# Branch products amid a chunked scan: an order written out by hand, one bank per chunk, decays from bfloat16 parts

## The chip, the cores and the metric

The kernel runs on one core of a Trainium2 chip. The metric is device time in microseconds for one execution. Before the change three runs took 2236.68, 2237.7 and 2242.37 us; the median is 2237.7. The engines go by their short names: PE is TensorE (PEld its weight loads), DVE VectorE, ACT ScalarE, POOL GpSimd, SP SyncE, whose queue issues the DMAs.

## What is computed

One layer of a hybrid decoder trunk on a sequence of 1024 positions and 1024 channels in float32. Three token mixers read one normalised input; each output goes through its own projection, the three are merged by sigmoid gates, an output projection follows, then a gated MLP.

```python
        y_ssm = ssm_mixer(z, xbc, dt_raw, ...)
        y_sb = stick_breaking_attention(sb_qkv)
        y_nsa = nsa_attention(nsa_q, nsa_kv, nsa_gate, ...)
        gm = jax.nn.sigmoid(merge_gate.astype(jnp.float32)).reshape(bsz, s, 3, D_MODEL)
        mixed = (gm[:, :, 0] * (y_ssm @ w_br_ssm[l]) + gm[:, :, 1] * (y_sb @ w_br_sb[l])
                 + gm[:, :, 2] * (y_nsa @ w_br_nsa[l])).astype(x.dtype)
        x = x + rms_norm(mixed @ w_out[l], post_mix_norm[l])
```

The first mixer's core is a scan over 8 chunks of 128 positions, with 16 heads in 4 groups that share B and C:

```python
    def step(state, inp):
        x_c, dt_c, b_c, c_c = inp
        acum = jnp.cumsum(dt_c * a, axis=1)
        seg = acum[:, :, None] - acum[:, None, :]
        decay = jnp.exp(jnp.where(tri, seg, -jnp.inf))
        cb = jnp.einsum('btgn,bsgn->btsg', c_c, b_c)
        w = cb[..., None] * decay * dt_c[:, None]
        y = jnp.einsum('btsgh,bsghp->btghp', w, x_c)
        y = y + jnp.einsum('btgn,bghpn->btghp', c_c, state) * jnp.exp(acum)[..., None]
        to_end = jnp.exp(acum[:, -1:] - acum) * dt_c
        state = (state * jnp.exp(acum[:, -1])[..., None, None]
                 + jnp.einsum('bsgh,bsghp,bsgn->bghpn', to_end, x_c, b_c))
        return state, y
```

Then a skip term D·x, a gate by silu(z), and a root-mean-square norm over each group's 256 channels.

## The kernel before

Activations lie with channels on the partitions and time on the free axis, in tiles of 128 x 512 or 128 x 1024. A large product of float32 data is made of three: both sides are split into a high part (rounded to fp32r) and the rest, and hi·hi, hi·lo and lo·hi add up in one PSUM bank. For a weight, ACT makes `whi` and POOL `wlo` (L287, L292, columns in pieces of 256). All products pass through two helpers at L219, so in the profile they share a line and are told apart by their tiles.

A scheduler decides the order of instructions on each engine at build time. Where `E.in_order[0]` is set, PE's products keep the order of the program; a `Fill` is a chain of branch or gate products of which `take(n)` writes out n steps at that point.

The stages follow each other: input projections into DRAM rows `s_d`; sparse attention (NSA), at whose end (L1103 to L1121) the scan's decays are made; stick-breaking attention (SB) with the last gate products amid it (`g_d`, written by SP from `gate_e`); `ssd_stage`; `tail_stage` with the branch projections, the output product and the MLP.

`ssd_stage` runs a `scan(q)` for each of the four groups; SSD_AT starts q = 0, 1 at slots 0 and 1, q = 2, 3 at 8 and 9, so that two scans run at a time. In a slot each running scan does `front(c+1)` and `back(c)`:

- `front` (L1294): a decay product `pseg` over 16 rows of fp32r (`half`, two parts of the cumulated decays, by `sel`), a bfloat16 product that adds the mask (`mask_d`), four ACT Exp with a bias (`dec`); transposes of x0, x1 and B, and B·C, into one ps_t bank; DVE `xd`, ACT `Bc`, POOL W = dec * Bc.
- `back` (L1318): C·state over 256 columns, which DVE turns into `yi` (times `eac`); Bc·xd for the new state; POOL and DVE update `state`; four W·xd of 64 x 128 and two ident·yi into the output bank; DVE adds D·x in place. State and output have a bank each (ps_b and ps_o for even q, two of the "dense" tag for odd).
- `norm` (L1346), after chunk 4 and at the end: POOL multiplies by the silu of z, ACT squares, POOL adds the two rows, a product with ones over 512 columns makes the mean square on all partitions, ACT and DVE make the root on 512 columns, and the result goes to `y_d` in DRAM.

No other products are written between these. The three branches come after (L1440). For NSA (rows 12 to 15 of `y_d`), SB (8 to 11) and SSM (0 to 7), each weight block j is loaded once for both halves of the sequence, and `ge`, a block of the gates, is loaded from `g_d`. NSA's result is kept in `lo` tiles, SB's is added by POOL (L1457), and the SSM rows come back from `y_d`.

## Time and profile before

| | us |
|---|---|
| median of 3 runs | 2237.7 |
| lowest, highest | 2236.68, 2242.37 |
| profiled execution, time | 2243.74 |
| profiled execution, span | 2242.0 |
| mean granted TensorE clock | 0.990 of full |
| HBM traffic over the span | 103 GB/s |

Times in the traces are counted from the span's start. In a row of groups stand line, engine, operation, output and inputs by the program's names, shapes, the count, busy time, the mean of one in ns, and the idle time just before them with what ended it. Matmuls overlap in the engine: a row's duration is longer than the distance to the next start. In a timeline row `x8` means eight instructions in a run, and a float32 product outside fp32r takes two instructions.

### The profile page before, as it was taken

How to read it: one execution, taken by the hardware profiler on the slowest of the kernel's cores; microseconds unless marked ns; L12 is line 12 of the kernel's file. 1: busy time of each engine (PE TensorE's matmuls, PEld its weight loads, DVE VectorE, ACT ScalarE, POOL GpSimd, SP SyncE). 2: the span in 40 equal slices, each digit the busy share in tenths (PEclk: the TensorE clock that was granted, in tenths of full speed). 3: DMA queues.
4: the chain of work that ended last, by engine and by line, in shares of the span. 5: the costliest groups of instructions: out<-in, count | busy, mean ns of one | idle time of the engine just before them, and what ended most of it. 6: DMA issues, size and time to landing. Idle time of an engine off the chain costs nothing.

```text
span 2242.0 us, 30070 instructions
## 1 busy us (share of the span) xinstructions
PE 2169.5 (97%) x10589; PEld 1733.7 (77%) x10589; DVE 1309.8 (58%) x2419; ACT 1199.5 (54%) x2236; POOL 1258.4 (56%) x1106
## 2 busy tenths in 40 slices
...
GB/s 174 82 113 108 111 130 61 111 83 36 41 88 36 11 59 38 63 60 65 123 209 69 85 239 145 85 109 176 117 92 80 118 94 109 100 193 171 141 105 117
DMA packets 119527, 232.53 MB, mean 104 GB/s; under 512 B 28752, under 2 KB 43024, under 8 KB 119376
## 3 DMA queue, kind: packets, MB, share of 16 engines
...
HBM read 167.00 MB, written 63.57 MB: 103 GB/s over the span
## 4 chain that ended last, share of the span: by engine, by line
PE 82%; DVE 5%; ACT 4%; POOL 3%; issue 3%; DMA 2%; SPq 0%; DVEq 0%; ACTq 0%; POOLq 0%
PE dense L219 56%; PE ps_s L219 7%; PE ps_o L219 7%; PE ps_t L219 6%; PE ps_b L219 4%; PE psn L219 2%; POOL wlo L538 0%; DMA wraw<-in_wfm 0%; ACT wT L1000 0%; POOL wlo L292 0%; DMA traw<-in_wtm 0%; DMA lo<-m_d 0%; POOL h_lo L472 0%; DVE x L1532 0%; DVE u L329 0%
## 5 line engine op out<-in xcount | busy, mean ns | idle before, releaser
L292 POOL TENSOR_TENSOR wlo<-wraw,whi 128x256 fp32r<-128x256 f32 x328 | 261.3, 827 | 281.5 <-ACT whi L287 270.2
L219 PE MATMUL dense<-h_hi,whi 128*128 128x512 f32 x656 | 262.6, 400 | 0.0
L219 PE MATMUL dense<-h_hi,wlo 128*128 128x512 f32 x656 | 256.8, 392 | 1.1 <-POOL wlo L538 1.1
L219 PE MATMUL dense<-h_lo,whi 128*128 128x512 f32 x656 | 256.7, 391 | 0.0
L1011 POOL TENSOR_TENSOR wT_lo<-wT,wT_hi 128x512 fp32r<-128x512 f32 x132 | 168.6, 1287 | 87.5 <-ACT wT_hi L1010 77.8
L219 PE MATMUL dense<-hi,whi 128*128 128x512 f32 x576 | 214.8, 392 | 0.3 <-ACT whi L287 0.3
L219 PE MATMUL dense<-hi,wlo 128*128 128x512 f32 x512 | 201.8, 396 | 0.4 <-POOL wlo L292 0.4
L219 PE MATMUL dense<-x,uhi 128*128 128x512 f32 x600 | 191.2, 391 | 2.9 <-ACT uhi L546 1.5
L219 PE MATMUL dense<-lo,whi 128*128 128x512 f32 x448 | 175.8, 393 | 0.0
L287 ACT ACTIVATE whi<-wraw 128x1024 fp32r<-128x1024 f32 (+1 forms) x90 | 88.4, 982 | 147.1 <-PE dense L219 117.7
L547 POOL TENSOR_TENSOR ulo<-uf,uhi 128x1024 fp32r<-128x1024 f32 x38 | 92.0, 2421 | 115.3 <-ACT uhi L546 113.4
L219 PEld LDWEIGHTS dense<-h_hi,wlo 128*128 128x128 f32 x656 | 123.2, 188 | 27.9 <-POOL wlo L538 1.5
L219 PEld LDWEIGHTS dense<-h_hi,whi 128*128 128x128 f32 x656 | 123.7, 189 | 23.4
L219 PEld LDWEIGHTS dense<-h_lo,whi 128*128 128x128 f32 x656 | 123.5, 188 | 22.7
L219 PEld LDWEIGHTS dense<-x,uhi 128*128 128x128 f32 x600 | 112.3, 188 | 28.3 <-ACT x L610 2.4
L1215 POOL TENSOR_TENSOR s_lo<-sa,s_hi 128x512 fp32r<-128x512 f32 (+2 forms) x48 | 53.6, 1118 | 139.8 <-ACT s_hi L1214 139.8
L219 PEld LDWEIGHTS dense<-hi,whi 128*128 128x128 f32 x576 | 108.4, 188 | 24.6 <-issue 1.4
L972 DVE TENSOR_REDUCE mx<-ps_t 128x1 f32<-128x384 f32 (+3 forms) x192 | 98.6, 520 | 49.3 <-PE ps_t L219 46.4
L329 DVE SCALAR_TENSOR_TENSOR u<-dense,pv,u 128x511 f32<-128x511 f32 (+1 forms) x140 | 103.4, 741 | 35.2 <-ACT u L325 35.1
L219 PEld LDWEIGHTS dense<-hi,wlo 128*128 128x128 f32 x512 | 96.6, 189 | 23.4 <-issue 1.9
L550 POOL TENSOR_TENSOR ulo<-uf,uhi 128x1024 fp32r<-128x1024 f32 x38 | 91.7, 2414 | 39.6 <-ACT uhi L549 37.8
L1000 ACT ACTIVATE wT<-ps_s 128x512 f32<-128x512 f32 x132 | 78.3, 595 | 60.5 <-PE ps_s L219 56.3
...
## 6 DMA issues: line engine op xcount, KB each, us to landing
wraw<-in_wfm SPq DMA_DIRECT2D x62, 512.0 KB, 3.7
wraw<-in_wup SPq DMA_DIRECT2D x50, 512.0 KB, 3.6
...
ge<-g_d SPq DMA_DIRECT2D x24, 512.0 KB, 3.4
...
row<-s_d SPq DMA_DIRECT2D x16, 512.0 KB, 4.6
```

What stands on the lines that cost most here:

```text
L219: i = f(*a, **k)
L287: act(hi, raw, AF.Copy)
L292: (V if tiles else P).tensor_tensor(lo[:, s], raw[:, s], fl(hi[:, s]), op=OP.subtract)
L329: V.scalar_tensor_tensor(o[:, d:], ps[:, :512 - d], taps[d], o[:, d:], op0=OP.mult, op1=OP.add)
L547: P.tensor_tensor(l24, f24, fl(h24), op=OP.subtract)
L550: P.tensor_tensor(l31, f31, fl(h31), op=OP.subtract)
L972: V.tensor_reduce(mx[:, h, a, n:n + 1], pm[:, :w], axis=AX, op=OP.max)
L1000: act(w.rearrange("p h q -> p (h q)"), pz, AF.Exp)
L1011: P.tensor_tensor(lo, wf, fl(hi), op=OP.subtract)
L1215: (P if SB_SLO else V).tensor_tensor(s_lo[:, c0:], a[:, c0:], fl(s_hi[:, c0:]), op=OP.subtract)
```

## The change

**Branch units inside the scan.** The 32 units of NSA and SB (two branches, two halves, eight blocks j) become a `Fill` of `ssd_stage`; PE keeps the program's order through the whole stage. From slot 1 on, two steps of it (k = two of four, six products) stand behind each front and each back. A weight block is loaded for each half, so 32 times instead of 16. The outputs go to ps_s.

**A chunk's outputs in one bank.** For c > 0 ACT makes exp of the decays over 512 columns, POOL multiplies it by C (`ce`), and four products state·ce of 64 x 128 go straight into the output bank before the four dec·xd; the state update has the bank's other half. `yi`, C·state and ident·yi go.

**Decays in bfloat16.** The cumulated decays are split into three bfloat16 parts (24 rows), so `pseg` is one bfloat16 product; no mask product: a Relu on ACT bounds the exponent, and DVE multiplies B·C by the triangle. DVE, not POOL, makes dec * Bc.

**Norms.** The sums over channels become products with one column of ones, the root is made on 128 x 4, spread by ACT and brought back by four transposes; result and split stay in SBUF (`E.ys`) in row and third tiles. `norm` falls into three pieces, of which the second and third come one and two slots later.

**SSM branch.** It stays behind the scan, by pairs of j and halves. SSD_ROWS sets the slots at which the rows of q = 2, 3 are loaded, in half tiles.

In the diff the removed lines of `ssd_stage` are left out; they stand in the kernel above.

```diff
+SSD_FROM = 1
+SSD_FILL = 2, 2
+SSD_LATE = 1, 0
+SSD_ROWS = {3: [(2, range(4), (0,))], 5: [(3, range(4), (0,))], 7: [(2, range(4), (1,)), (3, range(4), (1,))],
+            11: [(2, (4, 5), (0, 1)), (3, (4, 5), (0, 1))]}
...
-    ac_d = scratch("ac_d", [2, 8, 16, 128])
-    sel = keep.tile([16, 8], R32, name="sel")
-    V.tensor_tensor(sel, ident[0:16, 0:8], ident[0:16, 8:16], op=OP.add)
+    ac_d = dram.tile([3, 8, 16, 128], BF, name="ac_d", tag="ac_d")
+    sel = keep.tile([24, 8], BF, name="sel")
+    V.tensor_tensor(sel, ident[0:24, 0:8], ident[0:24, 8:16], op=OP.add)
+    V.tensor_tensor(sel, sel, ident[0:24, 16:24], op=OP.add)
...
-    act(E.nac.rearrange(fc), ps[:, :128], AF.Copy, scale=-1.0)
+    act(E.acu.rearrange(fc), ps[:, :128], AF.Copy)
...
+    tr(ps[:, 384:512], E.acu.rearrange(fc), ident)
+    ac = wk.tile([128, 128], F32, name="ac", bufs=1)
+    act(ac, ps[:, 384:512], AF.Copy, scale=-1.0)
+    for n in range(3):
+        b = wk.tile([128, 128], BF, name="ab", bufs=3)
+        act(b, ac, AF.Copy)
+        nc.sync.dma_start(E.ac_d[n].rearrange("c h t -> (c h) t"), b)
+        if n < 2:
+            V.tensor_tensor(ac, ac, b, op=OP.subtract)
...
         def front(c):
...
+            h, cs = c // 4, slice(c % 4 * 128, (c % 4 + 1) * 128)
+            pseg = E.ps_d()
+            mm(pseg, E.sel[:, c:c + 1].to_broadcast([24, 128]), ac, start=True, stop=True)
+            dec = wk.tile([128, 4, 128], F32, name="dec", bufs=3)
+            for n in range(4):
+                act(dec[:, n], pseg[:, n * 128:(n + 1) * 128], AF.Relu,
+                    bias=E.acu[:, c, 4 * q + n:4 * q + n + 1])
+            df = dec.rearrange("p h t -> p (h t)")
+            act(df, df, AF.Exp, scale=-1.0)
+            ce = None
+            if c > 0:
+                ce = ce_t()
+                act(ce.rearrange("p h t -> p (h t)"), pseg, AF.Exp, scale=-1.0)
+                P.tensor_tensor(ce, ce, C[h][:, None, cs].to_broadcast([128, 4, 128]), op=OP.mult)
             pt = ps_t()
             for n in range(2):
...
+                tr(pt[:, n * 128:(n + 1) * 128], xs[n][h][:, cs], ident)
+            tr(pt[:, 256:384], B[h][:, cs], ident)
+            mm(pt[:, 384:512], B[h][:, cs], C[h][:, cs], start=True, stop=True)
+            Bc = wk.tile([128, 2, 128], F32, name="Bc", bufs=3)
+            V.tensor_tensor(Bc[:, 1], pt[:, 384:512], E.tri_i, op=OP.mult)
+            act(Bc[:, 0], pt[:, 256:384], AF.Copy)
+            xd = wk.tile([128, 2, 4, 64], F32, name="xd", bufs=3)
             V.tensor_tensor(xd, pt[:, None, :256].rearrange("p a (h d) -> p a h d", h=4).to_broadcast([128, 2, 4, 64]),
                             E.dte[:, :, c, hs, None].to_broadcast([128, 2, 4, 64]), op=OP.mult)
...
+            V.tensor_tensor(dec, dec, Bc[:, 1:2, :].to_broadcast([128, 4, 128]), op=OP.mult)
+            return c, h, cs, xd, dec, ce, Bc
+        def back(c, h, cs, xd, W, ce, Bc):
+            bank = (ps_o if q % 2 else ps_b)()
+            po = [bank[(n % 2) * 64:(n % 2 + 1) * 64, (n // 2) * 128:(n // 2 + 1) * 128] for n in range(4)]
             if c > 0:
...
+                for n in range(4):
+                    mm(po[n], state[:, n, :], ce[:, n, :], start=n < 2, stop=False, skip_group_check=True)
+            for n in range(4):
+                mm(po[n], xd[:, 0, n, :], W[:, n, :], start=c == 0 and n < 2, stop=True, skip_group_check=True)
             if c < 7:
...
+                pst = bank[:, 256:512]
+                mm(pst, Bc[:, 0, :], xd[:, 1].rearrange("p h d -> p (h d)"), start=False, stop=True,
+                   skip_group_check=True)
                 if c == 0:
                     V.tensor_copy(sf, pst)
                 else:
                     P.tensor_tensor(state, state, E.eend[:, c, hs, None].to_broadcast([128, 4, 64]), op=OP.mult)
                     V.tensor_tensor(sf, sf, pst, op=OP.add)
...
             for n in range(2):
...
+                x = xs[n][h][:, cs]
+                V.scalar_tensor_tensor(x, x, pvc(PV_D, 2 * q + n), bank[:, n * 128:(n + 1) * 128],
                                        op0=OP.mult, op1=OP.add)
         def norm(h):
...
+            zs = [held[q][n][h] for n in (4, 5)]
             for n, z in enumerate(zs):
...
+                P.tensor_tensor(xs[n][h], xs[n][h], z, op=OP.mult)
+                act(z, xs[n][h], AF.Square)
+            later.append([SSD_LATE[0], sums, h, zs])
+        def sums(h, zs):
+            ps = ps_t()
+            for m, n in itertools.product(range(4), range(2)):
+                mm(ps[:, m:m + 1], zs[n][:, m * 128:(m + 1) * 128], E.ones[:, 0:1], start=n == 0, stop=n == 1)
+            r = wk.tile([128, 4], F32, name="r")
+            E.rsqrt_mean(r, ps[:, 4:8], ps[:, 0:4], 256)
+            rb = zs[0]
+            act(rb.rearrange("p (n t) -> p n t", t=128), r[:, :, None].to_broadcast([128, 4, 128]), AF.Copy)
+            later.append([SSD_LATE[1], out, h, zs, ps])
+        def out(h, zs, ps):
+            for m in range(4):
+                ms = slice(m * 128, (m + 1) * 128)
+                tr(ps[:, ms], zs[0][:, ms], ident)
+            for n, z in enumerate(zs):
+                V.scalar_tensor_tensor(z, xs[n][h], pvc(PV_SSM, 2 * q + n), ps, op0=OP.mult, op1=OP.mult)
+                hi, lo = [(E.third_t if q % 2 else E.row_t)(R32) for _ in range(2)]
+                act(hi, z, AF.Copy)
+                V.tensor_tensor(lo, z, fl(hi), op=OP.subtract)
+                E.ys[2 * q + n, h] = hi, lo
...
         for c in range(8):
             new = front(c + 1) if c < 7 else None
+            yield
             back(*st)
-            if c == 4:
-                norm(0)
+            if c % 4 == 3:
+                norm(c // 4)
             yield
             st = new
-        norm(1)
+            for x in list(later):
+                x[0] -= 1
+                if x[0] < 0:
+                    later.remove(x)
+                    x[1](*x[2:])
...
+    def rows(k0, h):
+        out = []
+        for k in range(4):
+            hi, lo = [yb.tile([128, 512], R32, name="y", bufs=16) for n in range(2)]
+            nc.sync.dma_start(fl(lo), E.y_d[(k0 + k) * 128:(k0 + k + 1) * 128, E.hs(h)])
+            act(hi, fl(lo), AF.Copy)
+            V.tensor_tensor(lo, fl(lo), fl(hi), op=OP.subtract)
+            out.append((hi, lo))
+        return out
...
+    def branches(ys):
+        units = [(br, h, j) for br in (2, 1) for h in range(2) for j in range(8)]
+        def load(br, h, j):
+            return E.load_w(A["wb_nsa" if br == 2 else "wb_sb"][j], 512)
+        ahead = [load(*units[0])]
+        ys = [ys]
+        for n, (br, h, j) in enumerate(units):
+            w = ahead.pop()
+            if n + 1 < len(units):
+                ahead.append(load(*units[n + 1]))
+            if j == 0:
+                y = ys.pop()
+            if j == 3:
+                nxt = {(2, 0): (12, 1), (2, 1): (8, 0), (1, 0): (8, 1)}.get((br, h))
+                ys = [rows(*nxt)] if nxt else []
+            e = E.row_t()
+            nc.sync.dma_start(e, E.g_d[(br * 8 + j) * 128:(br * 8 + j + 1) * 128, E.hs(h)])
+            out = []
+            yield from E.half_unit(Bank(), w, lambda k, _: y[k], 4, h, out)
+            if br == 2:
+                d = E.part[h, j] = E.lo_t(F32)
+                V.tensor_tensor(d, out[0], e, op=OP.mult)
+            else:
+                V.tensor_tensor(e, out[0], e, op=OP.mult)
+                P.tensor_tensor(E.part[h, j], E.part[h, j], e, op=OP.add)
     held = E.ssm
     gens = [None] * 4
...
+    acs = {q: ac_t(q) for q in range(2)}
+    E.ssm_rows(1, range(4), E.third_t, (0,))
+    fill = E.Fill(branches(rows(12, 0)))
+    E.ssm_rows(1, range(4), E.third_t, (1,))
+    E.ssm_rows(1, (4, 5))
+    E.in_order[0] = True
+    n = 0
+    while n == 0 or any(gens):
+        if n in SSD_ROWS:
+            for q, ns, h in SSD_ROWS[n]:
+                E.ssm_rows(q, ns, E.third_t if q % 2 and ns[0] < 4 else E.row_t, h)
         for q, at in enumerate(SSD_AT):
...
+            if n == at:
+                if q > 1:
+                    acs[q] = ac_t(q)
+                gens[q] = scan(q, *[held[q][m] for m in range(4)])
+            if gens[q]:
+                for m in range(2 if n > at else 1):
+                    if next(gens[q], 0) == 0:
+                        gens[q] = None
+                        break
+                    if n >= SSD_FROM:
+                        fill.take(SSD_FILL[m])
+        n += 1
+    E.in_order[0] = False
+    fill.rest()
...
+    for j0 in range(0, 8, 2):
...
+        for h in range(2):
+            for j, w, e in two:
+                ps, = fm_unit(psd, w, lambda k, h: E.ys[k, h], 8, halves=(h,))
...
```

How this moves instructions shows in three places. First PE in the steady scan. A slot of before, where `half,sel` and `ident_b,mask_d` are the decay product and its mask, `W,xd` a head's product, and `row_10833` and `third_11620` the C of the two scans:

```order
L219 MATMUL dense<-xd,Bc 128x256
L219 MATMUL ps_t<-ident,row_10827 128x128
L219 MATMUL ps_t<-ident,row_10829 128x128
L219 MATMUL ps_t<-ident,row_10831 128x128
L219 MATMUL ps_t<-row_10833,row_10831 128x128
L219 MATMUL ps_b<-state,row_10833 128x256
L219 MATMUL dense<-W,xd 64x128 x4
L219 MATMUL dense<-state,third_11620 128x256
L219 MATMUL ps_s<-half,sel 128x512
L219 LDWEIGHTS mask_d
L219 MATMUL ps_s<-ident_b,mask_d 128x512
L219 MATMUL ps_o<-W,xd 64x128 x4
```

The same part now, where `y` are the rows of a branch (whi and wlo its weights) and `ac` the three bfloat16 parts:

```order
L224 LDWEIGHTS sel
L224 MATMUL dense<-ac,sel 128x512
L224 MATMUL ps_t<-ident,row 128x128 x3
L224 MATMUL ps_t<-row 128x128
L224 MATMUL ps_s<-y,whi 128x512 x2
L224 MATMUL ps_s<-y,wlo 128x512
L224 MATMUL ps_s<-y,whi 128x512 x2
L224 MATMUL ps_s<-y,wlo 128x512
L224 MATMUL ps_b<-ce,state 64x128 x4
L224 MATMUL ps_b<-dec,xd 64x128 x4
L224 MATMUL ps_b<-xd,Bc 128x256
L224 MATMUL ps_s<-y,whi 128x512 x2
```

The mix of two scans that the scheduler had made has become one scan's front, six branch products, its back, and six more. The second place is the start of the stage. PE of before, at the last gate products (`h_hi`, `h_lo` with whi, wlo):

```order
L219 MATMUL dense<-h_hi,whi 128x512
L219 MATMUL dense<-h_lo,whi 128x512
L219 MATMUL dense<-h_hi,wlo 128x512
L219 MATMUL ps_s<-half,sel 128x512
L219 LDWEIGHTS mask_d
L219 MATMUL ps_s<-ident_b,mask_d 128x512
L219 MATMUL ps_o<-w_hi,row_10139 128x512
L219 MATMUL ps_o<-w_hi,row_10140 128x512
L219 MATMUL ps_o<-w_lo,row_10139 128x512
L219 MATMUL dense<-h_hi,whi 128x512
L219 MATMUL dense<-h_lo,whi 128x512
L219 MATMUL dense<-h_hi,wlo 128x512
```

And now, at the very last of them:

```order
L224 MATMUL dense<-h_hi,whi 128x512
L224 MATMUL dense<-h_lo,whi 128x512
L224 MATMUL dense<-h_hi,wlo 128x512
L224 LDWEIGHTS sel
L224 MATMUL dense<-ac,sel 128x512
L224 MATMUL ps_t<-ident,row 128x128 x3
L224 MATMUL ps_t<-row 128x128
```

A decay product that stood amid gates and the last SB product (`w_hi`, `w_lo`) now stands behind all gates. SP's queue around the same place, where `third` are rows of the second pair of scans' tiles, `y` the NSA rows and `gate_e` the last gates:

```order
L1250 DMA y_d<-ysb 128x512 x2
L585 DMA g_d<-gate_e 128x512
L687 DMA third<-s_d 128x512 x6
L1421 DMA y<-y_d 128x512
L687 DMA third<-s_d 128x512 x3
L290 DMA wraw<-in_wb_nsa 128x512
L585 DMA g_d<-gate_e 128x512
L687 DMA third<-s_d 128x512 x2
L1421 DMA y<-y_d 128x512
L687 DMA third<-s_d 128x512 x5
L1299 DMA ac<-ac_d 24x512 x2
L1421 DMA y<-y_d 128x512 x6
```

The loads of `ac` for q = 0 and 1 stand behind all sixteen half tiles `third` (the rows of q = 1 and q = 3) and behind the store of the last gates. The third place is the end of the scan on PE, now:

```order
L224 MATMUL ps_o<-ce,state 64x128 x4
L224 MATMUL ps_o<-dec,xd 64x128 x4
L224 MATMUL ps_o<-xd,Bc 128x256
L224 MATMUL ps_t<-ones,row 128x1 x8
L224 MATMUL ps_o<-ce,state 64x128 x4
L224 MATMUL ps_o<-dec,xd 64x128 x4
L224 MATMUL ps_t<-ident,row 128x128 x4
L224 MATMUL ps_t<-ones,row 128x1 x8
L224 MATMUL ps_t<-ident,row 128x128 x4
L224 MATMUL dense<-row,whi 128x512 x2
```

Where NSA's products stood behind the last chunks before, these last chunks and norms now run without branch products between them, and the first SSM product (`dense<-row,whi`) follows the last transposes. Outside the stretch from the end of the SB stage to the SSM branch, the order on every engine is unchanged.

229 lines of the change are left out of this document (72 added, 157 removed).

## The prediction

> **What bounds the kernel now.** I read the page's busy times first, then its chain of work, then windows over the stages that the change touches.
>
> ```profile
> PE 2169.5 (97%) x10589; PEld 1733.7 (77%) x10589; DVE 1309.8 (58%) x2419; ACT 1199.5 (54%) x2236; POOL 1258.4 (56%) x1106
> PE 82%; DVE 5%; ACT 4%; POOL 3%; issue 3%; DMA 2%; SPq 0%; DVEq 0%; ACTq 0%; POOLq 0%
> ```
>
> TensorE is busy for 97% of the span and carries 82% of the chain that ended last; nothing else has more than 5%. So a change pays where it takes products away or closes gaps between them. A busy figure alone can't tell a full engine, since the records of matmuls overlap. The windows (PE, weight loads, DVE, ACT, POOL, each with its count) say more:
>
> ```profile
> core 0: us, PE busy (x) PEld busy (x) DVE busy (x) ACT busy (x) POOL busy (x), PEclk, DMA share, GB/s
> 1158.00:1171.00 13.00, 10.73 (x56) 6.95 (x55) 5.04 (x12) 8.35 (x27) 6.36 (x7) 0.87 1.03 395
> 1171.00:1185.00 14.00, 14.00 (x97) 9.49 (x95) 7.79 (x19) 7.99 (x28) 9.28 (x10) 1.00 0.39 145
> 1185.00:1215.00 30.00, 29.13 (x193) 20.45 (x193) 23.39 (x55) 15.93 (x43) 21.26 (x21) 1.00 0.11 38
> 1215.00:1235.00 20.00, 17.95 (x85) 9.90 (x83) 12.22 (x25) 12.97 (x34) 13.32 (x11) 0.83 0.41 137
> 1235.00:1285.00 50.00, 48.47 (x308) 34.18 (x306) 34.92 (x76) 25.36 (x72) 34.42 (x32) 1.00 0.21 73
> 1285.00:1325.00 40.00, 39.72 (x176) 31.53 (x176) 23.59 (x36) 13.98 (x24) 13.95 (x17) 1.00 0.66 221
> 1325.00:1368.00 43.00, 42.64 (x188) 34.81 (x187) 23.50 (x24) 12.95 (x16) 37.53 (x32) 1.00 0.65 221
> 1368.00:1458.00 90.00, 90.00 (x387) 72.41 (x386) 25.32 (x31) 18.01 (x23) 47.69 (x50) 1.00 0.29 95
> ```
>
> The last row is dense TensorE: 387 products in 90 us, 0.233 us each. The NSA and SB products (1285 to 1368) run almost as densely. The scan's rows do not: the weight loads fall from 80% of the time to 50-70%, and the granted clock to 0.87 and 0.83. The stage to be judged has these ends:
>
> ```profile
> 1144.66 0.49 PE L219 MATMUL ps_s<-half,sel 16*128 16x512 f32 x1
> 1150.65 0.49 PE L219 MATMUL ps_s<-half,sel 16*128 16x512 f32 x1
> ...
> 1158.60 0.39 PE L219 MATMUL dense<-h_hi,wlo 128*128 128x512 f32 x1
> 1161.04 0.50 PE L219 MATMUL ps_s<-half,sel 16*128 16x512 f32 x1 [2.06 <-ACT dec L1302]
> ...
> 1368.62 0.40 PE L219 MATMUL dense<-yhi,whi 128*128 128x512 f32 x1
> ```
>
> The last gate product starts at 1158.60 and ends its turn at 1158.8; the first SSM-branch product starts at 1368.6. Scan plus two branches take **209.8 us**. All that comes earlier, and the SSM branch, the output product and the FFN behind it, keep their work, so the forecast is about these 209.8 us.
>
> **The change, part by part: TensorE's content.** What a product costs is the distance to the next start, not the printed duration:
>
> ```profile
> 1176.36 0.50 PE L219 MATMUL ps_s<-half,sel 16*128 16x512 f32 x1
> 1176.79 0.39 PE L219 MATMUL ps_s<-ident_b,mask_d 128*128 128x512 bf16 x1
> 1177.02 0.38 PE L219 MATMUL ps_t<-ident,row 128*128 128x128 f32 x2
> 1177.23 0.60 PE L219 MATMUL dense<-xd,Bc 128*128 128x256 f32 x2
> 1177.67 0.27 PE L219 MATMUL ps_t<-ident,row 128*128 128x128 f32 x1
> 1177.78 0.39 PE L219 MATMUL ps_t<-row,row 128*128 128x128 f32 x2
> 1178.09 0.66 PE L219 MATMUL dense<-W,xd 128*64 128x128 f32 x8
> 1178.68 0.71 PE L219 MATMUL dense<-ident,yi 128*128 128x128 f32 x4
> ```
>
> From start to start: the decay product over 16 rows 0.43; the bfloat16 mask of the same 512 columns 0.23; a float32 product of 256 columns (two passes) 0.44; a transpose, like any float32 pass of 128 columns, 0.11; four head products W·xd 0.59.
>
> There are 32 chunks (4 groups of 8), of which 28 have a state. Removed: 32 masks (7.4 us); on 32 decay products the step from 0.43 to the mask row's 0.23, since the new one is one bfloat16 pass over 512 columns (6.4); 28 C·state products (28 x 0.44 = 12.3); 28 pairs of ident·yi (four passes, 28 x 0.44 = 12.3); 8 norm sums over 512 columns, by twice the 256-column price 0.88 each (7.0). **45.4 us go.** Added: 28 sets of four ce·state with the shape of W·xd (28 x 0.59 = 16.5); 32 transposes in the norms (3.5); 64 column sums of one column, 128 passes. No row shows these. The lower bound is nothing; the upper is a whole 128-column pass, 0.11 each, 14 us, as weights are loaded for each. I take the middle, 7, because the nearest row loads the same weights but streams 128 columns more. **27 us come; net -18.4** (-25 to -11).
>
> What stays, besides: 384 branch products x 0.233 = 89.5, transposes 96 x 0.11 = 10.6, B·C 32 x 0.22 = 7.0, W·xd 32 x 0.59 = 18.9, state updates 28 x 0.44 = 12.3, and before the change 32 decay products at 0.43, 13.8. With the removed 39.0 (45.4 less the 6.4 already in those 13.8) that is 191; two decay products with their masks lie ahead of the stage (1144.66, 1150.65), so 190. **The stage now loses 209.8 - 190 = 20 us; after it has 171.5 of content and breaks even if it loses 38.**
>
> **The start, about 11.5 us.** The decay products that now hide among the gate products (1144.66, 1150.65) come behind the last of them, and TensorE's order is fixed there, so transposes and fill wait behind them. They need `ac`. In before's timeline SP issues the scan's rows from 1155.91 on; the list of transfers gives KB each and the median us to landing:
>
> ```profile
> 1155.91 5.07 SPq L679 DMA_DIRECT2D third<-s_d  x8
> ...
> third<-s_d SPq DMA_DIRECT2D x8, 512.0 KB, 7.5
> ```
>
> These 4 MB took the queue 7.5 us each to land. SP's new order puts `ac` behind the last gate's store and all 16 half tiles `third`, two `y` and one weight load, 19 transfers of 0.26 MB: 5.0 MB at 0.395 MB/us (first window) are 12.6 us after 1155.9. So `ac` lands near 1168.5, and TensorE, out of gates at 1158.8, stands for 9 to 10. Two more go to the first chunk's chain and a lowered clock (0.87 in this stretch already). Were the queue emptier, the wait would still hold until the last gate's sigmoid, three ACT passes of about 0.65 (L1352 below has their shape) after 1159, so 4 is the lower end; 16 the upper, if `y` lags too.
>
> **The middle, about 8 us.** Fill stands between every front and back, six products or 1.4 us; a chunk's back comes a whole slot after its front, nearly 11 us with two scans. What other engines do per chunk:
>
> ```profile
> L1302 ACT ACTIVATE dec<-ps_s,nac 128x128 f32<-128x128 f32 x128 | 36.4, 373 | 18.3 <-PE ps_s L219 11.4 <-POOL W L1315 6.5
> L1352 ACT ACTIVATE row<-row 128x512 f32<-128x512 f32 x8 | 5.2, 648 | 3.8 <-POOL row L1351 3.8
> L1310 DVE TENSOR_TENSOR xd<-ps_t,dte 128x512 f32<-128x512 f32 x32 | 21.8, 687 | 18.0 <-PE dense L219 10.7 <-PE ps_t L219 5.8 <-PE ps_b L219 1.3
> L1343 DVE SCALAR_TENSOR_TENSOR row<-row,pv,ps_o 128x128 f32<-128x128 f32 x32 | 9.6, 342 | 2.8 <-PE ps_o L219 2.6
> L1315 POOL TENSOR_TENSOR W<-dec,Bc 128x512 f32<-128x512 f32 x32 | 41.5, 1303 | 23.0 <-ACT Bc L1313 13.4 <-ACT dec L1302 9.5
> L292 POOL TENSOR_TENSOR wlo<-wraw,whi 128x256 fp32r<-128x256 f32 x34 | 27.9, 844 | 38.1 <-ACT whi L287 27.1 <-DMA g_d<-gate_e 11.0
> L1457 POOL TENSOR_TENSOR lo<-lo,ge 128x512 f32<-128x512 f32 x16 | 24.4, 1533 | 3.9 <-DVE ge L1455 3.1 <-PE dense L219 0.6
> L1331 POOL TENSOR_TENSOR state<-state,eend 128x256 f32<-128x256 f32 x24 | 14.7, 614 | 15.7 <-PE dense L219 9.9 <-PE ps_b L219 5.8
> L1351 POOL TENSOR_TENSOR row<-row,row 128x512 f32<-128x512 f32 x8 | 11.1, 1404 | 1.1 <-DVE row L1343 1.1
> L1354 POOL TENSOR_TENSOR row<-row,row 128x512 f32<-128x512 f32 x8 | 10.2, 1278 | 0.0
> ```
>
> ACT: four Relu 1.5, two Exp of 512 columns 1.3, a copy about 0.3: 3.1 per chunk. DVE: xd and the decay product 0.69 each, mask and two D terms 0.34 each, state 0.42: 2.8. Two chunks leave both some 5 of 11 us for units and norms, so the front's chain (1.5 + 0.65 + 1.3 for ce) is hidden by its slot; without that cover 3.5 us per chunk would show. A chunk's one bank is free again after two D terms and the state add, 1.1 us, and wanted a slot later. POOL is tighter, as the weights now come once per half: 32 loads in place of 16, their transfers hidden, their splitting doubled. In the scan's first half its ce (in W's place) and states leave time. In the second half, where the SB units run, its order holds 40 wlo, 16 adds, 15 ce, 13 states and 12 norm products: 40 x 0.844 + 16 x 1.533 + 15 x 1.303 + 13 x 0.614 + 12 x 1.404 = 102.7 us, against some 90 of TensorE. Weights are split one unit ahead and stand behind the adds in POOL's queue; TensorE's fixed order waits for them. About six of the twelve us should show, since the norms' POOL work reaches past the last unit; two more I allow the first half. Bounds 2 and 16.
>
> **The end, about 9.5 us.** The fill runs out two backs early, so q3's last chunk and norm have nothing between them: D terms 0.7, two POOL products 2.8, a Square 0.65, the column sums 0.8 (an eighth of the 7 above), two ACT and four DVE operations on four columns (no row shows one so small; at the 0.34 of a 128-column D term 2.0), a spread copy 0.65, transposes 0.45. That is 8 us, and 1.5 for the bare decay chain of the last chunk. The SSM products, fixed behind these transposes, start late. The norms' result stays on chip; the round trip that goes lay beside other work and gains nothing.
>
> **Sum:** 171.5 + 11.5 + 8 + 9.5 = 200.5, against 209.8: **-9.3 us**, the stage ending near 1359. The profiled execution took 2243.7 us (span 2242.0), 6 above the median of 2237.7; on the median's scale that gives 2228.4.
>
> The Trainium skill, "SBUF — State Buffer", section "SBUF: two separate sides", says that a DVE instruction with two SBUF inputs and a GpSimd one exclude each other for a whole instruction. That speaks against moving dec·Bc to DVE. The same 128x512 add on POOL takes 1278 (L1354) and 1533 ns (L1457), which would suit such a rule, though nothing in those rows names the other party. By it, an estimate, 32 new DVE products of 0.69 us would each hold POOL up, 11 us in the second half; the sum would then be about 2238, near POOL's rival below, which stands without it.
>
> **The rivals.**
> *POOL sets the pace of the second half.* If its operations stretch as the adds do (1533 against 1278, a fifth), ce and the norm products add 7 us to 102.7, 20 beyond TensorE's 90; less some 4 that the last norms' work may reach past the units, the middle costs 16, the total is 2236.4. For it: POOL is busy 37.5 of 43 us beside SB units already. Against: TensorE is busy 42.6 of those 43.
>
> *Slower: fixed order turns each late release into a stand.* Before, a late W let other ready products go first; now all, fill included, stand behind it. It decides from a mean of 0.3 us at each of the 64 places where a front or back begins: 64 x 0.3 = 19 in the middle, with start and end 40 in all, over the 38. At 0.4 the time is 2237.7 + (26 + 21 - 38) = 2246. For: scan rows of before lose 20 us even with free choice. Against: 1.4 us of fill per place, a slot of distance.
>
> *All latencies are covered but start and end.* Middle 0, end 8: 2219. For: the branches of before keep TensorE at 99% with POOL at 87%. Against: POOL's 102.7 above.
>
> *The narrow product is no cheaper.* A bfloat16 product over 24 rows keeps the 0.43 of the 16-row one: 6.4 us less gain, 2235. The mask row (0.23, same columns, bfloat16) speaks against.
>
> **How the numbers follow.** Forecast 0.45, POOL 0.2, fixed order 0.2, all covered 0.12, no cheaper 0.03. The range runs from 2212 (all covered, cheap column sums) to 2248 (fixed order at 0.4, a little over). A difference of 0.3%, 6.7 us, is about what a measurement of this kernel tells from none. Faster: 0.4 of the forecast's 0.45 and the covered case, 0.52; same: POOL's, the narrow product's and the forecast's short end, 0.28; slower: fixed order, 0.2.
>
> **What would show it.** Right: the new decay product 0.23 before the next start; first decay product near 1168, standing on a DMA; weight loads around 75% of the time between; SSM products starting near 1359 behind a gap of some 9 us that ends on ACT or POOL. Wrong: a start beyond 1172, waits on POOL wlo all through the SB units, or TensorE idle at every back. Anything that moves after the SSM branch would also make the sum wrong.

## The result, and the profile after

| | before | after |
|---|---|---|
| median, us | 2239.05 (2236.68 to 2242.37, 4 runs) | 2257.89 (2252.55 to 2260.36, 4 runs) |
| ratio, 95% interval | 1 | 1.0080 (1.0055 to 1.0105) |
| profiled execution, us | 2243.74 | 2255.84 |
| last gate product starts | 1158.60 | 1155.71 |
| first SSM product starts | 1368.62 | 1378.40 |
| stage between the two | 210.0 | 222.7 |

The kernel became slower by some 19 us, 0.8%. The forecast of 2228.4 has the wrong sign, and the range up to 2248 misses the time. The profiled execution of before was 4.7 us above its median, so the two profiles differ by 12.1 us only; the stage accounts for all of that (12.7). Gates end 2.9 us earlier, but in kernels with the same code up to there the last gate product starts anywhere from 1155 to 1159. Some 2 us are lost behind the stage: from the first SSM product to the end of the execution before takes 875.1 us and after 877.4 (875.8 to 879.0 in the kernels below that have the same code there). The other 6.7 us of the medians' difference are in no trace; the profiled execution of after lay 2.1 us below its median.

First the busy times from the page of after.

```profile
PE 2162.1 (96%) x10757; PEld 1735.9 (77%) x10757; DVE 1332.0 (59%) x2477; ACT 1228.7 (55%) x2327; POOL 1272.9 (56%) x1126
```

The page says almost nothing: TensorE's busy time fell by 7 us and the span grew by 12. The windows over the stage say where (PE, weight loads, DVE, ACT, POOL, clock, DMA share, GB/s):

```profile
1156.00:1173.00 17.00, 0.36 (x2) 0.10 (x1) 1.39 (x2) 3.60 (x6) 1.40 (x2) 0.58 0.95 331
1173.00:1180.00 7.00, 7.00 (x29) 4.83 (x28) 4.58 (x8) 6.11 (x17) 1.28 (x1) 0.56 0.41 150
1180.00:1350.00 170.00, 170.00 (x1109) 127.25 (x1107) 123.09 (x249) 102.26 (x271) 136.66 (x135) 0.99 0.39 122
1350.00:1378.00 28.00, 19.96 (x137) 16.37 (x138) 16.82 (x39) 13.13 (x32) 17.56 (x17) 0.74 0.21 75
```

Three things are to be seen. TensorE stands for nearly 17 us at the start, and the 7 us behind that run at a clock of 0.56. The 170 us in the middle are full: 170.00 busy, clock 0.99, no stand, POOL busy for 80%. And 8 of the last 28 us are empty, at a clock of 0.74. So the middle waits for nobody, and yet the stage is long.

The start, from the timeline, first PE's rows and then SP's:

```profile
1155.71 0.39 PE L224 MATMUL dense<-h_hi,wlo 128*128 128x512 f32 x1
1172.74 0.60 PE L224 MATMUL dense<-ac,sel 24*128 24x512 bf16 x1 [16.64 <-DMA ac<-ac_d]
1173.28 0.90 PE L224 MATMUL ps_t<-ident,row 128*128 128x128 f32 x3
...
```

```profile
1153.06 5.03 SPq L687 DMA_DIRECT2D third<-s_d  x6
...
1164.51 2.98 SPq L687 DMA_DIRECT2D third<-s_d  x5
1167.82 0.94 SPq L1299 DMA_DIRECT2D ac<-ac_d  x2
1169.13 3.83 SPq L1421 DMA_DIRECT2D y<-y_d  x6
```

Two loads of 24 KB, issued at 1167.82, are what TensorE waits for; they stand behind 16 tiles `third`, and the queue moved 331 GB/s where the forecast had 395 (225 up to 1162, 392 from there to 1172). Six of the `y` rows follow them.

The full middle, from the timeline: a slot of one scan, and behind the "..." of 1267 a norm's column sums.

```profile
1260.68 0.39 PE L224 MATMUL ps_s<-y,wlo 128*128 128x512 f32 x1
1261.00 0.66 PE L224 MATMUL ps_o<-ce,state 128*64 128x128 f32 x8
1261.49 0.61 PE L224 MATMUL ps_o<-dec,xd 128*64 128x128 f32 x8
1262.02 0.70 PE L224 MATMUL ps_o<-xd,Bc 128*128 128x256 f32 x2
1262.37 0.81 PE L224 MATMUL ps_s<-y,whi 128*128 128x512 f32 x2
1263.02 0.39 PE L224 MATMUL ps_s<-y,wlo 128*128 128x512 f32 x1
...
1263.72 0.40 PE L224 MATMUL ps_s<-y,wlo 128*128 128x512 f32 x1
1264.05 0.39 PE L224 MATMUL dense<-ac,sel 24*128 24x512 bf16 x1
1264.36 0.55 PE L224 MATMUL ps_t<-ident,row 128*128 128x128 f32 x3
...
1267.48 0.39 PE L224 MATMUL ps_s<-y,wlo 128*128 128x512 f32 x1
1267.71 1.84 PE L224 MATMUL ps_t<-ones,row 128*128 128x1 f32 x16
1269.41 0.71 PE L224 MATMUL ps_s<-y,whi 128*128 128x512 f32 x2
```

Read the distances between starts, and the array that each product uses (the pair with *). A branch product (`y,wlo`, 128\*128) ahead of the column sums, also 128\*128, takes its 0.23; ahead of `ce,state` (128\*64) it takes 0.32, ahead of the decay product (24\*128) 0.33. The decay product takes 0.31 before the transposes, where the forecast had the mask's 0.23. By these distances a change of the array's shape costs about 0.09; the experiments test that for the decay product. The two passes behind the back's last product take 0.65 (1262.37 to 1263.02) in place of 0.46. And the 16 passes of the column sums take 1.70 us, 0.106 each: as much as a pass with 128 columns.

The end, from the timeline:

```profile
1356.68 2.79 POOL L297 TENSOR_TENSOR wlo<-wraw,whi 128x256 fp32r<-128x256 f32 x4
...
1359.43 3.38 POOL L1367 TENSOR_TENSOR row<-row 128x512 f32<-128x512 f32 x2
...
1363.53 3.14 PE L224 MATMUL ps_t<-ones,row 128*128 128x1 f32 x14 [1.29 <-ACT row L1368]
...
1369.05 2.49 POOL L1367 TENSOR_TENSOR third<-third,row 128x512 f32<-128x512 f32 x2 [3.99 <-DVE third L1360]
...
1372.59 3.15 PE L224 MATMUL ps_t<-ones,row 128*128 128x1 f32 x14 [0.97 <-ACT row L1368]
...
1377.63 1.11 PE L224 MATMUL ps_t<-ident,row 128*128 128x128 f32 x4 [1.90 <-ACT row L1378]
1378.40 1.20 PE L224 MATMUL dense<-row,whi 128*128 128x512 f32 x2
```

Two norms stand bare here, where the forecast had one; the first one's products wait on POOL behind four pieces of a weight's splitting, and at the lowered clock 14 of a norm's 16 passes take 3.1 us.

### The profile page after: what moved, and what is told of

Read it like the earlier page. It is cut to its first block, busy times and chain, and to the rows that moved or that the text cites. A ratio compares the mean times of both kernels' runs of the same rounds, so it can differ in the third digit from the quotient of the medians.

```text
span 2254.1 us, 30683 instructions
## 1 busy us (share of the span) xinstructions
PE 2162.1 (96%) x10757; PEld 1735.9 (77%) x10757; DVE 1332.0 (59%) x2477; ACT 1228.7 (55%) x2327; POOL 1272.9 (56%) x1126
## 4 chain that ended last, share of the span: by engine, by line
PE 84%; DVE 4%; ACT 4%; issue 3%; DMA 3%; POOL 3%; SPq 0%; DVEq 0%; ACTq 0%; POOLq 0%
PE dense L224 54%; PE ps_s L224 10%; PE ps_t L224 7%; PE ps_o L224 6%; PE ps_b L224 4%; PE psn L224 2%; DMA third<-s_d 0%; POOL wlo L543 0%; ACT wT L1010 0%; DMA wraw<-in_wfm 0%; DMA lo<-m_d 0%; POOL h_lo L477 0%; DVE u L334 0%; POOL wlo L297 0%; ACT wT_hi L1020 0%
## 5 line engine op out<-in xcount | busy, mean ns | idle before, releaser
L297 POOL TENSOR_TENSOR wlo<-wraw,whi 128x256 fp32r<-128x256 f32 x360 | 288.5, 830 | 266.7 <-ACT whi L292 266.4
L224 PE MATMUL dense<-hi,wlo 128*128 128x512 f32 x448 | 176.8, 396 | 0.7 <-POOL wlo L297 0.7
L224 PE MATMUL dense<-hi,whi 128*128 128x512 f32 x448 | 175.3, 391 | 0.0
L292 ACT ACTIVATE whi<-wraw 128x1024 fp32r<-128x1024 f32 (+1 forms) x106 | 99.1, 935 | 106.7 <-PE dense L224 85.7
L543 POOL TENSOR_TENSOR wlo<-wraw,whi 128x1024 fp32r<-128x1024 f32 x38 | 92.9, 2444 | 29.7 <-ACT whi L542 29.5
L224 PE MATMUL dense<-hi,uhi 128*128 128x512 f32 x248 | 98.0, 395 | 6.8 <-ACT snap L1625 5.6
```

The costliest lines, as they stand in the source:

```text
L224: i = f(*a, **k)
L292: act(hi, raw, AF.Copy)
L297: (V if tiles else P).tensor_tensor(lo[:, s], raw[:, s], fl(hi[:, s]), op=OP.subtract)
L543: P.tensor_tensor(wlo, raws[0], fl(whi), op=OP.subtract)
```

## The experiments

Every kernel ran in turn with the one before on the same chip; ratios are to that one, with 95% intervals. The first eight ask which part of the stage is long and what it is worth.

**The decay parts loaded early** (`ac` of two scans into lasting memory at the end of the NSA stage):

```diff
-    acs = {q: ac_t(q) for q in range(2)}
+    # at the end of the NSA stage
+    for q in range(2):
+        E.acs[q] = E.ac_t(q)
```

> The two loads of `ac` for the first pair of scans are issued at the end of the NSA stage instead of behind the sixteen loads of `third`; the dead `eac` goes. In the changed kernel's trace TensorE stands 16.8 us (1155.9 to 1172.7) until `ac` lands, and 3 more are lost to a lowered clock. Theory A (the wait is for `ac` alone): the first decay product comes within 1 us of the last gate product and nearly all of it goes, total 15 us or more below the changed kernel (2243 or less). Theory B (the wait is for the whole burst of loads, and `ac` is only the last of it that TensorE meets): after one or two decay products and their transposes TensorE stops again, for `y`, whose first two rows were used by ACT at 1163.9 and 1169.1; the first branch products come near 1170 instead of 1176, and the total falls by 3 to 6 us (about 2253).

Measured: 2256.05, ratio 1.0074 (1.0056 to 1.0092). The first decay product follows the gates at once, at 1155.47, and then TensorE stands for `y`, as PE's timeline of this kernel shows:

```profile
1156.56 0.37 PE L224 MATMUL dense<-ac,sel 24*128 24x512 bf16 x1
...
1164.99 1.52 PE L224 MATMUL ps_s<-y,whi 128*128 128x512 f32 x2 [7.36 <-ACT y L1424]
...
1171.80 0.79 PE L224 MATMUL ps_s<-y,whi 128*128 128x512 f32 x1 [4.86 <-ACT y L1424]
```

The start still loses 18 us: theory B. The small load was only the first thing to come late; the whole burst is too late. The middle has the same products as after. From the 5th to the 29th decay product it takes 147.0 us here and 148.5 in after, where the clock falls to half for 3.4 us near 1232. The 147.0 is what the next kernels without such a dip are to be compared with.

**One row of squares in the norms** (POOL adds two squared rows; 8 column passes in place of 16 per norm):

```diff
+            P.tensor_tensor(zs[0], zs[0], zs[1], op=OP.add)
-            for m, n in itertools.product(range(4), range(2)):
-                mm(ps[:, m:m + 1], zs[n][:, ...], E.ones[:, 0:1], start=n == 0, stop=n == 1)
+            for m in range(4):
+                mm(ps[:, m:m + 1], zs[0][:, ...], E.ones[:, 0:1], start=True, stop=True)
```

> POOL adds the two squared rows first, so a norm takes 8 column-sum passes instead of 16. Theory A (each pass of one column costs as much as a whole 128-column pass, 0.112 us in the trace, bound by its weights): a norm's sums take 0.92 us instead of 1.84, 8 norms give 7.4 us back, 2 more at the end where the clock is low, against about 3 at the end for two more POOL adds of 1.3 us in the bare tail; total 5 to 8 us below the changed kernel (about 2251). Theory B (the sums were cheap and their 21.8 us are waiting): no change in the middle, and the tail longer by the adds, total 0 to 3 us above.

Measured: 2257.80, 1.0074 (1.0059 to 1.0089). From the 5th to the 29th decay product it takes 142.9 us in place of 148.5, or of 147.0 without the dip of the clock. The groups of after and of this kernel between 1180 and 1345 us, after first:

```profile
L224 PE MATMUL ps_t<-ones,row 128*128 128x1 f32 x80 | 9.2, 245 | 0.0
```

```profile
L224 PE MATMUL ps_t<-ones,row 128*128 128x1 f32 x40 | 4.8, 242 | 0.2 <-POOL row L1369 0.2
```

Forty passes less save 4.1 us, 0.10 each, about the 4.4 that their own rows show. So the sums' price is that of full passes, as theory A had it. The gain is lost in the bare end, where POOL has one more operation per norm: from the last `y` product to the first SSM product it takes 30.7 us instead of 25.4.

**Longer fill blocks, half as many:**

```diff
-SSD_FILL = 2, 2
+SSD_FILL = 4, 0
```

> Fill of four steps (12 products) behind each front and none behind each back: the same products, half as many changes between branch products and scan products. Theory A (a change of kind costs TensorE time by itself, about 0.2 us for going in and out, since the first weights of the next kind load only when the product before is done: the last product before a scan product keeps its place 0.32 instead of 0.23 us and the first behind it is longer too): 30 changes fewer, 5 to 6 us less between 1180 and 1350, total about 2252. Theory B (the branch products' 103 instead of 89.5 us are small waits for operands): nothing gained, or a loss, since a back now follows straight on the other scan's work without fill and its waits are no longer covered; total 2257 or more.

Measured: 2255.62, 1.0063 (1.0048 to 1.0078). The stretch of decay products takes 148.7 us, without a dip of the clock and with 12 more branch products in it, 2.8 us of work: some 1 us is gained on the 147.0, where theory A had 5 to 6. So the number of blocks is not what costs: from the last pass of the chunk product `xd,Bc` straight to the decay product the distance is 0.31 too, against 0.22 for such a pass among like ones, and fewer blocks leave the number of shape changes as it was.

**SSM products as fill in the tail:**

```diff
+        for j in range(2):
+            w = E.load_w(A["wb_ssm"][j], 1024)
...
+            yield from E.half_unit(Bank(), w, lambda k, _: E.ys[k, 0], 8, 0, out)
```

> Two SSM units of the first half (48 products, 11 us) are written as further fill behind the NSA and SB units, so the last chunks have products between them; the same products are left out of the SSM branch, their weights are loaded once more. In the changed kernel the stretch from 1350 to 1380 loses 14 us. Theory A (the end is bare latency: POOL products, squares, sums, root, transposes in a row, with the clock falling): the fill covers the wait before the last backs and half of the norms, 6 to 9 us gained, total about 2250; the last norm of q = 3 stays bare, some 7 us. Theory B (POOL, still busy with weights and adds until 1360, is late, and sets the end whatever TensorE does): the last transposes come no earlier than 1376, the 48 products only move in front, and the gain is their 11 us all the same unless POOL's additional splitting (8 pieces, 6 us) delays the norms by as much; then 5 us or less is gained.

Measured: 2264.05, 1.0100 (1.0085 to 1.0115), worse than after. SSM products need the thirds that the last norms make, and the last norm of all still stands bare (PE's timeline of this kernel):

```profile
1391.46 0.59 PE L224 MATMUL ps_t<-ones,row 128*128 128x1 f32 x2 [6.04 <-ACT row L1368]
```

**All loads of the start in a written order** (the first experiment's early `ac`, and the first `y` rows pinned ahead of `third`):

```diff
+            if (k0, h) == (12, 0):
+                tc.keep_in_program_order(i)
...
+    E.load_order[0] = True
+    first = rows(12, 0)
```

> As the run with the early `ac` (it stopped again behind 3 us of work, at `y`: 14.0 us lost up to 1170 and 17.9 to 1190, against 16.8 and 19.8), but the four `y` rows of the first half are issued ahead of all `third`, and the rows of q = 3 keep their place in the program. Theory A (the burst behind which the loads queue is the cause, whichever load is met first): four `y` and eight `third`, 3.1 MB at 0.36 to 0.4 MB/us from 1153, are there by 1161; TensorE loses 3 to 6 us at the start instead of 18 to 20, and the total falls by 12 to 15 us, to about 2243. Theory B (the memory that the SB stage gives back, not the queue, decides when loads begin, or the scans' other rows are late by as much): the loss stays over 12 us and moves to the third or fourth decay product.

Measured: 2254.73, 1.0059 (1.0040 to 1.0078). The start's loss falls from 18 to 12.6, and neither theory fits whole: pinned, the `y` loads stand behind the last gates' store (SP's timeline, then PE's).

```profile
1162.18 0.42 SPq L585 DMA_DIRECT2D g_d<-gate_e  x1
1162.70 1.89 SPq L1425 DMA_DIRECT2D y<-y_d  x4
```

```profile
1169.61 0.80 PE L224 MATMUL ps_s<-y,whi 128*128 128x512 f32 x1 [7.72 <-ACT y L1428]
```

**The norms' gating products on DVE:**

```diff
-                P.tensor_tensor(xs[n][h], xs[n][h], z, op=OP.mult)
+                V.tensor_tensor(xs[n][h], xs[n][h], z, op=OP.mult)
```

> The two products of a norm (y times the silu of z, 128x512) go from POOL to DVE; nothing else differs from the changed kernel. There, the last ce of q = 3 was ready at 1358.6 and POOL began it at 1363.8, behind four pieces of an SSM weight (2.8 us), two norm products (3.4) and the state (1.1). Theory A (POOL's queue sets the end): the last back comes 3 us earlier and the last norm's products, 2 x 0.7 instead of 2 x 1.25, save one more; the first SSM product comes 3 to 5 us earlier counted from the last gate product, total about 2253. Theory B (TensorE's fixed order and the chain of the norm set it, POOL only fills the time): no change of the end, and 11 us more DVE in a middle where DVE is 75% busy cost up to 2 us.

Measured: 2255.37, 1.0070 (1.0055 to 1.0085); the stage 219.8, 2.9 less: 3.7 at the end, less a little at the start. The middle is 148.5 us as in after, each with one dip of the clock, so POOL did not pace it.

**Part of the fill kept back for the end** (one step in place of two behind the backs of eight slots):

```diff
-                        fill.take(SSD_FILL[m])
+                        fill.take(1 if m and 4 <= n < 12 else SSD_FILL[m])
```

> The same products, but behind the backs of slots 4 to 11 one step of fill instead of two, so that 16 steps (48 products, 11 us) are left for the last slots. Theory A (the end is a chain of waits during which TensorE has nothing written): the middle shortens by 11 us, the end grows by less, since its gaps (14 us from 1350 to 1380) take 48 products in; 5 to 9 us earlier, total about 2250. Theory B (POOL is the bound of the end, as in the run with SSM units there, which lost 18 us in spite of its fill): the SB adds and weights now fall into the end as well and push the norms' POOL products back, gain 3 us or less.

Measured: 2258.78, 1.0088 (1.0072 to 1.0105): no gain. The last `y` product starts at 1370.8 instead of 1353.0, and from there to the first SSM product it takes 10.3 us instead of 25.4; the last norm stays bare. But the middle gives up what the end gains. Between 1190 and 1340 us the granted clock is 0.95, against 0.99 in after: it falls to half three times, which costs 7 us instead of 2, and 1.3 us are a wait. Why the clock falls there is not shown.

**The last three together:**

> The three together: loads in order, norm products on DVE, fill kept for the end. If the start, POOL's queue and the bare end are separate causes, the gains add: 13 + 4 + 6 = 23 us less than the changed kernel, about 2234, below the kernel before (2241.7). If the end is one chain that only moves, the sum falls short by the smaller parts: 2240 to 2244.

Measured: 2245.14, 1.0026 (1.0016 to 1.0036, 9 runs). The start now loses 12.7 us and the end, 8.2 us long, some 5; some 5 more are lost in between, 2.2 of them in waits for `xd` and 1.7 at half clock. That is 23 in all, where the forecast allowed 29. Still the stage is 209.6 us long, against 210.0 of before, whose trace lay above its median: by the medians this kernel is 5.4 slower. **A stage that loses less than the forecast allowed is no shorter than the old one: TensorE's content did not fall by 18.4.** The next four ask why.

**The decay product over all 128 rows**, 104 of them zero, else after:

```diff
-    sel = keep.tile([24, 8], BF, name="sel")
+    sel = keep.tile([128, 8], BF, name="sel")
...
-        ac = wk.tile([24, 512], BF, name="ac")
-        nc.sync.dma_start(ac, E.ac_d[...])
+        ac = wk.tile([128, 512], BF, name="ac")
+        V.memset(ac, 0.0)
+        nc.sync.dma_start(ac[:24], E.ac_d[...])
...
-            mm(pseg, E.sel[:, c:c + 1].to_broadcast([24, 128]), ac, start=True, stop=True)
+            mm(pseg, E.sel[:, c:c + 1].to_broadcast([128, 128]), ac, start=True, stop=True)
```

> The decay product takes 128 rows, of which 104 are zeros, instead of 24; nothing else differs from the changed kernel. There the product behind it starts 0.316 us later and it starts 0.329 us after a branch product, where a bfloat16 product of as many columns and the branch products among themselves take 0.23; the long-fill run has shown that the number of fill blocks is not the cause. Theory A (every change of the shape that the array is used in, 128*128 to 24*128 and back, costs 0.09 us, since the weights of the new shape are not loaded behind the running product): both numbers become 0.23, 0.18 us per chunk, 4 to 4.5 us less from the fifth to the twenty-ninth decay product (148.5 us), total 5 to 6 below the changed kernel (about 2252). Theory B (the change between bfloat16 and float32 products costs it): both stay over 0.31, no gain.

Measured: 2250.31, 1.0053 (1.0037 to 1.0068), 7.6 us below after (by the two ratios, 6.0). PE's timeline of this kernel, to be laid beside 1263.72 to 1264.36 of after:

```profile
1259.32 0.40 PE L224 MATMUL ps_s<-y,wlo 128*128 128x512 f32 x1
1259.56 0.39 PE L224 MATMUL dense<-ac,sel 128*128 128x512 bf16 x1
1259.79 0.49 PE L224 MATMUL ps_t<-ident,row 128*128 128x128 f32 x3
```

The product with five times the rows is cheaper: 0.23 instead of 0.31 to the next start, and 0.24 instead of 0.33 ahead of it. The first transpose behind it takes 0.11 instead of 0.17. From the 5th to the 29th decay product it takes 141.4 us instead of the 147.0 of this code without a dip of the clock. The 5.6 are 0.23 for each of 24 chunks, about what the three distances add up to (0.09, 0.09 and 0.06). That is the shape's price by itself.

**All together** (the three, 128 rows, `y` unpinned, and the squares and ones of the norms in bfloat16):

```diff
-                act(z, xs[n][h], AF.Square)
+                act(z.bitcast(BF)[:, :512], xs[n][h], AF.Square)
```

> As the run of three together (2245.1), with decay products over 128 rows, squares and the column of ones in bfloat16 (the squares lose precision, the sums are one pass of bfloat16 each instead of two of float32), and the first `y` loads no longer pinned behind the last gate's store. Expected from the parts: 5.5 for the shape, 64 fewer passes of 0.115 plus whatever a bfloat16 weight load is shorter, 7 to 10, and 3 to 5 at the start (first branch product near 1162 instead of 1166.6, counted from gates that end at 1156.5): 15 to 20 us below it, 2226 to 2230, that is 10 to 14 below the kernel before. If the content is not what the change lost (a rival: the time is lost in waits of other engines that merely move when TensorE gets shorter, POOL's first), it gains 8 or less: 2237 or more.

Measured: 2239.82, 1.0000 (0.9991 to 1.0009, 11 runs); level with before, where 2226 to 2230 had been worked out. In the profiled execution, 3.2 us below the median, the stage is 200.0 us; the part from the first SSM product on takes 878.4, 3 more than before's 875.1. So of the 10 us by which the two traces' stages differ, 3 are lost behind the stage, and the rest is that before's trace lay above its median and this one below. PE's timeline and the waits between 1158 and 1358 us (engine, tile, what it waited for: us, times, longest):

```profile
1253.24 0.35 PE L224 MATMUL ps_t<-ones_b,row 128*128 128x1 bf16 x8
1253.46 0.71 PE L224 MATMUL ps_s<-y,whi 128*128 128x512 f32 x2
```

```profile
PE ps_t L224 <- DVE xd L1342: 9.8, 7, 3.4
PE ps_b L224 <- DVE dec L1344: 5.7, 1, 5.7
PE ps_t L224 <- ACT row L1385: 4.0, 1, 4.0
```

Eight bfloat16 passes take 0.22 us, 0.028 each, against 0.106 for a float32 one. But with TensorE shorter, DVE is late: it now holds the norms' products as well, and TensorE stands for its `xd` seven times.

**The norms' products on POOL again for the first two groups, else the same:**

```diff
-                V.tensor_tensor(xs[n][h], xs[n][h], z, op=OP.mult)
+                (P if q < 2 else V).tensor_tensor(xs[n][h], xs[n][h], z, op=OP.mult)
```

> As the run of all parts together (2239.8), but the norm products of the first pair of scans (q = 0, 1) go back to POOL; those of q = 2, 3 stay on DVE. In that run TensorE waited 9.8 us in seven places for DVE's xd, DVE being 83% busy over the sampled windows, while POOL was 50 to 60% busy between 1230 and 1260. Theory A (DVE had become the bound in places): four of the seven waits, 8.5 us of the losses between 1210 and 1280, go; total 2232 to 2235, below the kernel before by 0.2 to 0.3%. Theory B (the waits come from rows that land late, since the loads are pinned, and DVE only shows the transposes' bank): no gain, 2238 or more.

Measured: 2238.78, 0.9996 (0.9987 to 1.0005, 11 runs). The windows and the waits:

```profile
1200.00:1350.00 150.00, 138.61 (x985) 104.39 (x989) 124.48 (x247) 95.71 (x249) 121.34 (x119) 0.99 0.39 125
```

```profile
PE ps_t L224 <- DVE xd L1342: 9.2, 6, 2.3
```

The wait stayed, so the products of those two groups were not its cause. DVE is busy for 83% and POOL for 81%, with the order fixed on all engines; which of DVE's other operations holds `xd` up was not tried.

**The kernel before with its decay product over 128 rows**, nothing else:

```diff
-    sel = keep.tile([16, 8], R32, name="sel")
+    sel = keep.tile([128, 8], R32, name="sel")
...
-        ac = E.hd.tile([128, 512], R32, name="half")[:16]
+        ac = E.hd.tile([128, 512], R32, name="half")
+        V.memset(fl(ac), 0.0)
```

> The kernel before, with its decay product (fp32r, `half` and `sel`) over 128 rows, of which 112 are zeros, instead of 16; nothing else differs. There it takes 0.43 us to the next start, while other fp32r products of 512 columns take 0.23. Theory A (the rule of the shape that the run with 128 rows showed in the changed kernel holds here too, and the forecast's 6.4 us for a narrower type were really a price of the shape): the distance falls to 0.23, and the 0.31 ahead of it to 0.22, 0.3 us for each of 32 chunks, 9 us of TensorE; of this the part shows in which TensorE, not ACT, is late: 3 to 8 us, total 2232 to 2237. Theory B (fp32r with few rows is slow by itself, or the scan waits for other engines anyway): less than 2 us.

Measured: **2233.38** (2231.47 to 2234.80, 6 runs), ratio 0.9965 (0.9952 to 0.9978): 7.1 us faster than before, and the fastest of all that ran. The stage is 202.7 us in place of 210.0, the part behind it unchanged at 875.2. The same place in the timelines of before and of this kernel:

```profile
1181.79 0.60 PE L219 MATMUL dense<-state,third 128*128 128x256 f32 x2
1182.31 0.49 PE L219 MATMUL ps_s<-half,sel 16*128 16x512 f32 x1
1182.73 0.39 PE L219 MATMUL ps_s<-ident_b,mask_d 128*128 128x512 bf16 x1
```

```profile
1177.62 0.60 PE L219 MATMUL dense<-state,third 128*128 128x256 f32 x2
1177.86 0.58 PE L219 MATMUL ps_s<-half,sel 128*128 128x512 f32 x1
1178.29 0.39 PE L219 MATMUL ps_s<-ident_b,mask_d 128*128 128x512 bf16 x1
```

From `state,third` to the mask it takes 0.94 us before and 0.67 here; over 32 chunks the 0.27 make 8.6 us, near what the time and the stage show. In this place only the sum can be read, since the full decay product is listed 0.03 behind the pass ahead of it and so still stands 0.43 before the mask. Where the decay product stands behind a gate product, it starts 0.32 us after that one in before and 0.23 here, and its own distance to the mask falls as well (before, then this kernel):

```profile
1144.66 0.49 PE L219 MATMUL ps_s<-half,sel 16*128 16x512 f32 x1
1145.08 0.39 PE L219 MATMUL ps_s<-ident_b,mask_d 128*128 128x512 bf16 x1
```

```profile
1143.41 0.39 PE L219 MATMUL ps_s<-half,sel 128*128 128x512 f32 x1
1143.64 0.39 PE L219 MATMUL ps_s<-ident_b,mask_d 128*128 128x512 bf16 x1
```

So 16 rows cost 0.09 ahead and 0.19 behind.

## Why the prediction was wrong, step by step

**The step that failed is the content's sum, "27 us come; net -18.4".** The mean distance to the next start between 1182 and 1350 us (the median for transposes), times the count of the whole stage, against the forecast's terms:

| | forecast, us | measured each | us |
|---|---|---|---|
| 384 branch products | 89.5 | 0.264 | 101.5 |
| 128 column-sum passes | 7.0 | 0.108 | 13.8 |
| 32 decay products | 7.4 | 0.316 | 10.1 |
| 28 sets ce·state | 16.5 | 0.50 | 14.1 |
| 32 sets dec·xd | 18.9 | 0.56 | 17.9 |
| 28 xd·Bc, 32 B·C | 19.3 | 0.35, 0.14 | 14.4 |
| 128 transposes | 14.1 | 0.110 | 14.1 |
| sum | 172.7 | | 185.9 |

(The 172.7 is the forecast's 171.5 with two decay products that it left out; they used to stand among the gates.) The content is 186 us, 14.4 more than forecast. That is about 4 less than the 190 that the forecast had worked out for before from single rows, not 18.4 less. Three terms were too small.

- *Column sums "the middle, 7": the largest, 6.8 too little.* They cost the upper bound, 14: one column takes as long as 128, in float32. The nearest row, by the text's own rule, was the transpose with the same weights; the middle was no reading of it.
- *The decay product's step "from 0.43 to the mask row's 0.23 (6.4)": 2.7 too little.* The mask row has 128 rows, the new product 24. The 24-row product takes 0.09 more on either side, as the full-rows kernel shows, and the first transpose behind it 0.06 more, 1.8 us in all that the table's median leaves out. The 0.43 of before was dear for its 16 rows: filled up to 128 it frees 0.27 per chunk. So the rival given 0.03, "the narrow product is no cheaper", came near: of the 0.20 per product 0.11 came, and the transpose gave 0.06 of that back. The reason is the rows, not the type.
- *Branch products at 0.233 each: with the scan's sets beside them 3.7 too little.* 0.233 is their price in a dense row of like products. Here 64 places of the written order set products of other shapes beside them. Some 50 of their blocks end ahead of a decay product or a set of ce·state or dec·xd, at 0.32 to 0.33 for the last product, 4 to 5 us together. Most of the other 7 us of the 12 is only a matter of where a start is listed: the first product behind a back or a front takes longer (the 0.65 above), and xd·Bc and B·C ahead of it take less than their 0.44 and 0.22. Branch products, sets, xd·Bc and B·C together are 147.9 us against 144.2; some 1.5 of that is the dip of the clock.

The decay product's share is tested by an edit in two kernels, the column sums' by halving their passes. For the sets of 64 columns (128\*64) the 0.09 is read from the timeline alone.

The Trainium skill, "TensorEngine Tiling (Array Packing)", section "Key Properties", says that changing the tiling mode drains TensorE. A price at each change of shape, 0.09 us for the 24-row product, would suit that; the page gives no price, and no run here shows that it is a drain. The Trainium skill, "TensorE: Matmul & The Clock Gate", section "LDWEIGHTS (loading the stationary operand)", lets a weight load take its columns over 1.2 in ns, 107 ns for 128, an estimate from the page. The 0.108 of a float32 column-sum pass agree; the 0.028 of a bfloat16 pass with as many columns, in the kernel with all together, lie far below it.

**The start, 11.5 forecast, 19.8 measured.** The cause was right (SP's order, `ac` behind 16 tiles), the size was not: 16.8 us of standing instead of 9 to 10. The gates ended 2.9 us earlier, and the first decay product came at 1172.7 instead of 1168.5, since the queue moved 331 instead of 395 GB/s and the load of `ac`, issued at 1167.8, still had its own landing behind that; and 3 more at the low clock behind it (7 us at 0.56 lose 44%), to which the forecast gave part of 2. It is above the upper bound of 16.

**The middle, 8 forecast, 3 measured** (what is left of the stage). None of it is a stand: TensorE is busy for 170.00 of 170 us. POOL was busy for 80% of them, and TensorE waited for none of it. Both rivals in which TensorE waits fall here: POOL did not set the pace (moving 16 of its products changed nothing there), and the fixed order made no stands at 64 places. What the fixed order did cost came through the shapes it sets side by side. When the content is shortened, as in the last but one kernel, waits for DVE do show, 9 us: the middle's cover is thin. POOL's state operation grew from 614 to 878 ns, and TensorE stood for none of it. The prediction's estimate of 2238 went by the rule of the Trainium skill, "SBUF — State Buffer", section "SBUF: two separate sides", that such a DVE instruction and a GpSimd one exclude each other; that time did not show, and whether the rule stretched the operation no run tells.

**The end, 9.5 forecast, 14 measured** (what the 25.4 us from the last branch product to the first SSM product take beyond the products' prices in the middle). Two bare norms, POOL's splitting ahead of them, column sums at 3.1 us instead of 0.8 by full passes and a lower clock.

Together, in the stage: 14.4 of content (185.9 less 171.5), 8.3 at the start and 4.5 at the end too little, 5 in the middle too much: 22.2 us, from 200.5 to the measured 222.7. The 2 us behind the stage were no term of the forecast. The break-even was put at a loss of 38; at the true content it lies at 24, and the stage loses 37. With the losses alone put right the sum would have been 171.5 + 37 = 208, level with before; the content made it slower.
